# Eight weight operands of the second layer's MLP prepared one layer early and kept in DRAM

## The chip, the cores and the metric

The kernel runs on one core of one Trainium2 chip. Its time is the device time of one execution in microseconds (us). The comparison is between the medians of several executions; a profiled execution is a separate one.

## The reference

A trunk of two layers works on 1024 tokens of width 1024. Layer 0 mixes tokens by latent attention, layer 1 by a chunkwise mLSTM; each mixer is followed by a gated MLP. What the change touches is that MLP's first product, `h @ w_up`:

```
h = rms_norm(x) * (1 + sc_f) + sh_f
a, g = split(h @ w_up, 2)                 # w_up: 1024 x 5632, a and g 2816 wide
a = causal_depthwise_conv3(a) + conv_b
x = x + g_f * ((gelu(a) * g) @ w_down)
```

Everything is float32.

## The kernel before

**Three matmuls for one product.** A float32 operand is split in two: `hi`, its rounding to the fp32r format, made by ScalarE (ACT, line 1019), and `lo`, the rest, made by VectorE (DVE, line 1020). `mm3` (lines 178 to 180) adds up hi by hi, hi by lo and lo by hi on TensorE (PE).

**Seven products for eight.** An up pass (`mlp`, called once for each layer) works on 22 groups `m`. A group has 128 columns of `a` and 128 of `g`; the tokens come in two halves and the inner dimension in two halves, so a plain scheme has eight block products. The kernel uses seven, in a form with sums and differences of blocks. They are numbered 1 to 7: `p1` to `p7` run them, `w_a`, `w_s1`, `w_s3`, `w_s4` and small lambdas (together `weights_of`) make their weight operands. Operand 1 and 2 are the two halves of the `a` weights (`ra`) as they are; 5 is the sum of the halves of the `g` weights (`rg`, line 1033); 3, 6 and 7 derive from sums and differences (lines 1039, 1040, 1044); 4 is a half of `rg`. One product is 12 matmuls of 128x128 by 128x512. The seven activation operands are called B11, B21 (these come straight from `h`), T1, B22, T2, T3 and T4; the last five come from `operands_second`, whose DVE work is on lines 937, 969, 977, 981, 987 and 944.

**Order.** `sequence` lists the products as items. The first eight items of a pass are the operands 1 and 2 of groups 0 to 3 (`AHEAD = 4`), since their activations are ready first; then come 5, 5, 3, 3, 6, 6, 7, 7 of groups 0 and 1, then 5, 5, 4, 4 and so on. A loop at the end of `mlp` makes operands ahead of the product that runs: up to `LOOK` = 7 items ahead for the first eight and 5 after that. Since groups 0 to 3 come back later for operands that need `ra`, they load it again (`again`). The order of instructions on each engine is laid down at compile time by a planner with its own costs: it goes by the order of the program and fills an engine's gap with later work that it takes to be ready. At run time each engine keeps that order.

**Buffers.** Operands live in pairs in tiles `w0` and `w1` (hi and lo); there are four such tiles (`wbufs`), so eight operands. A tile comes free when both of its products have run. Raw weights have five tiles `raw`, the sums two tiles `wsum`.

**Stores for later.** In layer 0's up pass, between its products, 28 items make the weight operands of layer 1's output projection (four groups of seven) and write hi and lo to DRAM (`spill_units`, `wo_d`, by SyncE's (SP) queue); `SPILL = (47, 21)` puts them in four lots of seven, the first at item 47, with 21 products between two lots. Their raw weights and sums live in four rooms of one tile `sp`. Also from item 28 on, at every fourth item, `extra` does one of 24 dot products of the modulation (line 216).

**Where layer 1's up pass begins.** `OutProj` reads its stored operands back by GpSimd's queue (POOL, line 1373), two lots of products ahead, into the same `w0`/`w1` tiles. After its last products (`oa`) come layer 1's up products at once (`pa`, `pb`, `pd`). A few matmuls into them PE forms the sum of squares of the second half of the tokens (`st`, line 268), DVE and POOL make the reciprocal root of it (`rstd`, line 273), PE spreads it over the partitions (`rb`, line 280), and then `operands_second` can begin.

Of the kernel before, what the change touches and what calls it, by code (L numbers as in the profile page):

```python
# [11 lines left out]
F32 = mybir.dt.float32  # L12
F32R = mybir.dt.float32r
# [5 lines left out]
P = 128  # L19
# [4 lines left out]
HS = 512  # L24
# [63 lines left out]
U_MV0 = (U_MV, U_MV + 1, U_MG)  # L88
# [12 lines left out]
def trunk_kernel(ctx: ExitStack, tc: tile.TileContext, xT, pos, c_d, cols_d, mod_w, win, winT, w0, w1, wf, wd, out):  # L101
# [4 lines left out]
    def nm(s):  # L106
        n_names[0] += 1
        return f"{s}_{n_names[0]}"
# [23 lines left out]
    def block(i, shape, dt, name):  # L132
        return blk.tile(shape, dt, tag=f"b{i}", name=nm(name))
# [758 lines left out]
    def store_x(l, hf, m, x):  # L892
        nc.sync.dma_start(x_d[l][hf][m], x[:, m, :])
# [99 lines left out]
    def home(px, i, dt, name):  # L993
        return (px if i > 5 else blk).tile([P, KT, HS], dt, tag=f"b{i}", name=nm(name))

    def mlp(px, psC, T, l, u_d, pd, done, cols, extra=None, scaled=None, store=None, more=None, spill=None, homes=(6, 0)):

# [23 lines left out]
        def weights_of(raw, room_for=None):  # L1023

            def w_a(g):
                g["ra"] = raw(g["m"], 0)
                return wop(g["ra"][:, 0:HS], dve)

            def w_s1(g):
                g["rg"] = raw(g["m"], 1)  # L1030
                t = room_for() if room_for else wp.tile([P, 1024], F32, tag="wraw", bufs=wraws, name=nm("wsum"))
                g["s"], g["t"] = t[:, 0:HS], t[:, HS:]
                dve.tensor_tensor(g["s"], g["rg"][:, 0:HS], g["rg"][:, HS:], ALU.add)
                return wop(g["s"], dve)

            def w_s4(g):
                if g["again"]:
                    g["ra"] = raw(g["m"], 0)
                dve.tensor_tensor(g["s"], g["s"], g["ra"][:, 0:HS], ALU.subtract)
                dve.tensor_tensor(g["t"], g["ra"][:, HS:], g["s"], ALU.subtract)  # L1040
                return wop(g["t"], dve)

            def w_s3(g):
                dve.tensor_tensor(g["t"], g["ra"][:, 0:HS], g["rg"][:, 0:HS], ALU.subtract)
                return wop(g["t"], dve)

            return {1: w_a, 2: lambda g: wop(g["ra"][:, HS:], dve), 3: w_s4, 4: lambda g: wop(g["rg"][:, HS:], dve),
                    5: w_s1, 6: lambda g: wop(g["s"], dve), 7: w_s3}

        def prod(ps, w, t, first, T=T):  # L1050
# [69 lines left out]
        def sequence(groups, made, run):  # L1120
# [5 lines left out]
            for n in range(AHEAD, len(groups)):  # L1126
# [5 lines left out]

        seq = sequence([{"m": m, "again": m < AHEAD} for m in range(FT)], weights_of(raw),
                       {1: p1, 2: p2, 3: p3, 4: p4, 5: p5, 6: p6, 7: p7})
        if spill is not None:
            rooms = []

            def room_for():
                if not rooms:
                    t = block(2, [P, 4, 1024], F32, "sp")  # L1140
                    rooms.extend([t[:, i, :] for i in range(4)])
                rooms.append(rooms.pop(0))
                return rooms[-1]

            made = weights_of(lambda m, i: spill[0](room_for(), m, i), room_for)
            for n, g in enumerate({"m": m, "again": False} for m in range(4)):
                at = SPILL[0] + n * (SPILL[1] + 7)
                seq[at:at] = [(lambda k=k, g=g: made[k](g), lambda w, k=k, g=g: spill[1](k, g["m"], w))
                              for k in (1, 2, 5, 3, 6, 7, 4)]
        ends = {k: len(seq) - 1 - i for i, k in enumerate((4, 7, 6, 3, 0, 2, 0, 1, 5))}  # L1150
        hooks = {}

# [181 lines left out]

    REST = (7, 8, 10)
    DOTS = 28
    SPILL = (47, 21)
    pF = []
    ORD = (("B11", "B21", "T1", "B22", "T2", "T3", "T4"),) * 2 + (("B11", "T1", "T2", "B22", "T3", "B21", "T4"),)

# [147 lines left out]
    def mixer_products(weights_of, prod, bank, sequence, hook):  # L1488

        def unit_raw(m, i):  # L1490
            t = px.tile([P, 1024], F32, tag="raw", bufs=RAWS, name=nm("raw"))
            nc.sync.dma_start(t, w1[PAIRS[m][i]])
            return t

        def held(tag, shape, bufs):
            return pD[0].tile(shape, F32, tag=tag, bufs=bufs, name=nm("c"))[:, 0:HS]

        def scale_of(g):
            return KSCALE if g["m"] < MH else 1.0

        def result(g, row, hf, t):
            u = PAIRS[g["m"]][row]
            if u >= U_MO:
                og_form(t)
                nc.sync.dma_start(og_d[u - U_MO][hf], t)
            else:
                nc.sync.dma_start(qk_d[g["m"]][row][hf], t)

        def p1(g, w):
            g["A"] = mm_tile("ma")  # L1510
            prod(g["A"], w, "B11", True, hT)
            g["a1"] = held("raw1", [P, 1024], 4)
            with tc.high_priority():
                act.activation(g["a1"], g["A"], AF.Copy)

        def p2(g, w):
            b = bank("mb")
            prod(b, w, "B21", True, hT)
            with tc.high_priority():
                dve.tensor_tensor(g["a1"], g["a1"], b, ALU.add)  # L1520
            result(g, 0, 0, g.pop("a1"))

        def p5(g, w):
            g["D"] = bank("md")
            prod(g["D"], w, "T1", True, hT)
            g["g2"] = held("g2", [P, HS], 2)
            with tc.high_priority():
                act.activation(g["g2"], g["D"], AF.Copy, scale=scale_of(g))

        def p3(g, w):  # L1530
            prod(g["D"], w, "B22", False, hT)
            g["a2"] = held("raw1", [P, 1024], 4)
            with tc.high_priority():
                act.activation(g["a2"], g["D"], AF.Copy)

        def p6(g, w):
            prod(g["A"], w, "T2", False, hT)
            with tc.high_priority():
                dve.tensor_tensor(g["a2"], g["a2"], g["A"], ALU.add)
            result(g, 0, 1, g.pop("a2"))  # L1540

        def p7(g, w):
            prod(g["A"], w, "T3", False, hT)
            with tc.high_priority():
                dve.scalar_tensor_tensor(g["g2"], g["A"], scale_of(g), g["g2"], ALU.mult, ALU.add)
            result(g, 1, 1, g.pop("g2"))

        def p4(g, w):
            prod(g["A"], w, "T4", False, hT)
            t = held("raw1", [P, 1024], 4)  # L1550
            with tc.high_priority():
                act.activation(t, g["A"], AF.Copy, scale=scale_of(g))
            result(g, 1, 0, t)

        def b12():
            t = block(1, [P, KT, HS], F32R, "B12")
            hT["B12"] = t[:, 0:4], t[:, 4:8]
            for k in (0, 2):
                r = px.tile([P, 1024], F32, tag="raw", bufs=RAWS, name=nm("raw")).rearrange("p (k t) -> p k t", k=2)
                for i in range(2):  # L1560
                    nc.sync.dma_start(r[:, i, :], b12_d[k + i])
                split_two(hT["B12"], k, r)

        vps = []

        def v_first(j, w):
            if j == 0:
                need(hT["B11"])
                vps.extend(mm_tile("vf") for _ in range(4))
            for k in range(3 * j, min(3 * j + 3, KT)):  # L1570
                for t in range(4):
                    mm3(vps[t][:, 0:264], [x[:, k, t * P:(t + 1) * P] for x in hT["h"]], wk(w, k % 3, 264),
                        k == 0, k == KT - 1)
            if j == 2:
                v = pD[0].tile([P, 1024], F32, tag="raw1", bufs=4, name=nm("v"))
                with tc.high_priority():
                    for t in range(4):
                        act.activation(v[:, t * 256:(t + 1) * 256], vps[t][:, 0:256], AF.Copy)
                        dve.tensor_copy(gtok[:, :, t], vps[t][:, 256:264])
                nc.sync.dma_start(va_d, v)  # L1580

        n = len(PAIRS)
        for i in REST:
            hook(i + 3, lambda: (need(hT["T1"]), piece(hT["rest"])))
        hook(n * 7 - 2, b12)
        return [(lambda j=j: unit(w1[U_MV0[j]]), lambda w, j=j: v_first(j, w)) for j in range(3)] + sequence([{"m": m, "again": m < AHEAD} for m in range(n)], weights_of(unit_raw),
                        {1: p1, 2: p2, 3: p3, 4: p4, 5: p5, 6: p6, 7: p7})

    pD = []
    mlp(px, psC, T, 0, u_d[0], pD, done, ((0, HS),), lambda i: piece(mods, i >= DOTS and i % 4 == 0),  # L1590
        store=lambda hf, m, x: store_x(1, hf, m, x), more=mixer_products, spill=spill_units(1, w1, U_OUT1))
    for _ in mods:
        pass

# [366 lines left out]
    def done(hf, t0, w, x, ssq):  # L1961
# [2 lines left out]

    pD = []
    mlp(px, psC, T, 1, u_d[1], pD, done, ((0, 256), (256, 256)), lambda i: piece(mods, i >= 60 and i % 6 == 0), gain,
        homes=(0, 6))
    need(xs)
    stP.close()
    pD[1].close()  # L1970
# [98 lines left out]
```

## Time and profile before

| | |
|---|---|
| median of three executions | 2167.46 us (2167.31 to 2170.86) |
| the profiled execution's own time | 2169.14 us |
| its span, first to last instruction | 2167.4 us |
| PE busy | 2134.8 us, 98% of the span |
| DVE busy | 1770.3 us, 82% |
| ACT busy | 1078.4 us, 50% |
| POOL busy | 71.2 us, 3% |

The profile gives for each engine the time in which it had an instruction in work. PE's matmuls overlap, so a busy PE can still run below its pace; the number of matmuls in a stretch tells that. In a row of the view of the instructions in order of time there stand the start, the duration, the engine, the line, the operation, the tiles written and read, the shapes, the count, and in brackets how long the engine had been idle and what ended that. In the view by windows a row has the stretch and its length, then for each engine the busy time and the number of instructions, then the granted share of TensorE's clock, the busy share of the DMA engines and the GB/s that they moved.

### The profile page before, as it was taken

How to read it: one execution, taken by the hardware profiler on the slowest of the kernel's cores; microseconds unless marked ns; L12 is line 12 of the kernel's file. 1: busy time of each engine (PE TensorE's matmuls, PEld its weight loads, DVE VectorE, ACT ScalarE, POOL GpSimd, SP SyncE). 2: the span in 40 equal slices, each digit the busy share in tenths (PEclk: the TensorE clock that was granted, in tenths of full speed). 3: DMA queues.
4: the chain of work that ended last, by engine and by line, in shares of the span. 5: the costliest groups of instructions: out<-in, count | busy, mean ns of one | idle time of the engine just before them, and what ended most of it. 6: DMA issues, size and time to landing. Idle time of an engine off the chain costs nothing.

```text
span 2167.4 us, 28571 instructions
## 1 busy us (share of the span) xinstructions
PE 2134.8 (98%) x10401; PEld 1792.1 (83%) x10401; DVE 1770.3 (82%) x2837; ACT 1078.4 (50%) x1797; POOL 71.2 (3%) x164
## 2 busy tenths in 40 slices
PE   9999999999999999999999999999999999999998
PEld 7878888787888888878888889988788888887887
DVE  8877778669899987899988477787986777779988
ACT  5465566446555554433365464445644444453335
POOL 0000000000000000000000011021000000000000
PEclk9999999999999999999999999999999999999999
DMA  8512334842466652552144444486233332246212
GB/s 321 165 45 58 98 101 151 271 142 90 141 225 228 228 204 88 187 179 81 59 165 149 157 151 151 144 291 224 77 133 97 112 125 90 77 156 220 66 54 78
DMA packets 130700, 313.23 MB, mean 145 GB/s; under 512 B 14528, under 2 KB 22272, under 8 KB 130560
## 3 DMA queue, kind: packets, MB, share of 16 engines
q1 hardware_dynamic: 126128, 296.33, 41.3%
q0 software_dynamic: 4032, 14.68, 2.1%
q8 instruction: 82, 1.34, 0.3%
q14 instruction: 58, 0.48, 0.1%
q10 hardware_dynamic: 400, 0.39, 0.1%
HBM read 242.24 MB, written 65.96 MB: 142 GB/s over the span
## 4 chain that ended last, share of the span: by engine, by line
PE 84%; DVE 7%; DMA 4%; issue 2%; ACT 2%; SPq 1%; POOL 1%; POOLq 0%; DVEq 0%; ACTq 0%
PE pa L178 7%; PE pa L180 7%; PE pa L179 7%; PE pd L180 4%; PE pd L178 4%; PE pd L179 4%; PE sc L698 4%; PE da L178 3%; PE da L179 3%; PE da L180 3%; PE db L178 2%; PE db L180 2%; PE db L179 2%; PE pb L180 2%; PE pb L178 2%
## 5 line engine op out<-in xcount | busy, mean ns | idle before, releaser
L178 PE MATMUL pa<-T,whi 128*128 128x512 f32 x528 | 206.0, 390 | 0.0
L179 PE MATMUL pa<-T,whi 128*128 128x512 f32 x528 | 205.6, 389 | 0.0
L180 PE MATMUL pa<-T,wlo 128*128 128x512 f32 x528 | 205.2, 389 | 0.0
L1019 ACT ACTIVATE whi<-wsum 128x512 fp32r<-128x512 f32 x196 | 120.1, 626 | 137.6 <-PE pa L179 53.1
L1020 DVE TENSOR_TENSOR wlo<-wsum,whi 128x512 fp32r<-128x512 f32 x196 | 132.1, 686 | 29.8 <-ACT whi L1019 28.3
L179 PE MATMUL da<-U,whi 128*128 128x512 f32 (+1 forms) x364 | 139.1, 382 | 0.0
L178 PE MATMUL da<-U,whi 128*128 128x512 f32 (+1 forms) x364 | 139.1, 382 | 0.0
L1019 ACT ACTIVATE whi<-raw 128x512 fp32r<-128x512 f32 x147 | 88.7, 623 | 101.3 <-PE pb L179 49.4
L180 PE MATMUL da<-U,wlo 128*128 128x512 f32 (+1 forms) x364 | 138.7, 382 | 0.0
L1238 ACT ACTIVATE whi<-raw 128x1024 fp32r<-128x1024 f32 (+1 forms) x60 | 59.2, 987 | 133.5 <-PE da L179 56.8
L1020 DVE TENSOR_TENSOR wlo<-raw,whi 128x512 fp32r<-128x512 f32 x147 | 99.6, 686 | 23.8 <-ACT whi L1019 23.8
L178 PEld LDWEIGHTS pa<-T,whi 128*128 128x128 f32 x528 | 99.2, 188 | 21.8 <-DVE a L1105 0.7
L180 PEld LDWEIGHTS pa<-T,wlo 128*128 128x128 f32 x528 | 99.3, 188 | 20.7
L179 PEld LDWEIGHTS pa<-T,whi 128*128 128x128 f32 x528 | 99.2, 188 | 20.6
L1064 ACT ACTIVATE ct<-a,cols 128x512 f32<-128x512 f32 x88 | 70.9, 810 | 80.2 <-DVE a L1086 46.1
L180 PE MATMUL db<-U,wlo 128*128 128x512 f32 x264 | 102.7, 390 | 1.7 <-DVE wlo L1239 1.7
L178 PE MATMUL db<-U,whi 128*128 128x512 f32 x264 | 103.3, 391 | 0.8 <-ACT whi L1238 0.8
L179 PE MATMUL db<-U,whi 128*128 128x512 f32 x264 | 102.9, 390 | 0.0
L1189 ACT ACTIVATE U<-q 128x1024 fp32r<-128x1024 f32 x84 | 79.9, 979 | 45.4 <-DMA q<-ud 15.9
L1190 DVE TENSOR_TENSOR U<-q,U 128x1024 fp32r<-128x1024 f32 x84 | 94.2, 1130 | 5.3 <-ACT U L1189 5.3
L1065 DVE SCALAR_TENSOR_TENSOR ct<-a,cols,ct 128x512 f32<-128x512 f32 x88 | 65.6, 748 | 18.4 <-ACT ct L1064 18.4
L178 PEld LDWEIGHTS da<-U,whi 128*128 128x128 f32 x364 | 68.4, 188 | 13.9 <-ACT whi L1238 0.7
(486 smaller groups left out, 6231.1 us busy)
## 6 DMA issues: line engine op xcount, KB each, us to landing
raw<-in_wf SPq DMA_DIRECT2D x96, 512.0 KB, 4.2
mraw<-in_mod_w SPq DMA_DIRECT2D x56, 512.0 KB, 4.1
wraw<-in_w SPq DMA_DIRECT2D x44, 512.0 KB, 3.5
ud<-ct SPq DMA_DIRECT2D x88, 256.0 KB, 2.1
q<-ud SPq DMA_DIRECT2D x88, 256.0 KB, 4.7
raw<-in_wd SPq DMA_DIRECT2D x32, 512.0 KB, 4.2
pa<-in_mod_w SPq DMA_DIRECT2D x24, 512.0 KB, 3.6
x<-xd SPq DMA_DIRECT2D x48, 256.0 KB, 4.6
```

The lines of the kernel that those rows point to most:

```text
L178: pe.matmul(ps, lh, rh, start=first, stop=False, skip_group_check=more)
L179: pe.matmul(ps[:, 0:rl.shape[-1]], lh, rl, start=False, stop=False, skip_group_check=more)
L180: pe.matmul(ps, ll, rh, start=False, stop=last, skip_group_check=more)
L698: pe.matmul(ps[:, cs], a[:, qs if n < 3 else qrs_], b[:, cs], start=n == 0, stop=n == 4)
L1019: act.activation(hi, src, AF.Copy)
L1020: eng.tensor_tensor(lo, src, hi.bitcast(F32), ALU.subtract)
L1064: act.activation(t, a[:, 2:], AF.Identity, bias=col(f"cb{l}", m), scale=cw(m, 2))
L1065: dve.scalar_tensor_tensor(t, a[:, 1:HS + 1], cw(m, 1), t, ALU.mult, ALU.add)
L1189: act.activation(hi, w, AF.Copy)
L1190: dve.tensor_tensor(lo, w, hi.bitcast(F32), ALU.subtract)
L1238: act.activation(hi, src, AF.Copy)
```

## The change

Operands 1 and 2 of groups 0 to 3 of layer 1's up pass, its first eight items, are no longer made there. They are made in layer 0's up pass as eight more items (36 in all) and stored in DRAM (`ff_d`, by `ff_store`); layer 1 reads them back by POOL's queue (`ff_first`), two operands at a time into one pair of tiles. The 36 items come in six lots of six, the first at item 42, with 14 products between two lots; the four groups of seven are now cut across the lots, and the eight new items come last. The raw weights of the new items come into the same four rooms of `sp`. `w_g2` loads `rg` where a group has not loaded it; here every group that uses operand 4 has. What stands as `seq = ...; return seq` in `mixer_products` is only written differently.

```diff
+        if first is not None:
+            seq[:len(FIRST)] = [(lambda i=i: first(i), seq[i][1]) for i in range(len(FIRST))]
         if spill is not None:
-            rooms = []
...
-            made = weights_of(lambda m, i: spill[0](room_for(), m, i), room_for)
-            for n, g in enumerate({"m": m, "again": False} for m in range(4)):
-                at = SPILL[0] + n * (SPILL[1] + 7)
-                seq[at:at] = [(lambda k=k, g=g: made[k](g), lambda w, k=k, g=g: spill[1](k, g["m"], w))
-                              for k in (1, 2, 5, 3, 6, 7, 4)]
+            items = list(spilled(weights_of, spill[:2], 2, spill[2]))
+            for n in range(SPILL[2]):
+                m = len(items) // SPILL[2]
+                at = SPILL[0] + n * (SPILL[1] + m)
+                seq[at:at] = items[n * m:n * m + m]
...
-    SPILL = (47, 21)
+    SPILL = (42, 14, 6)
+    FIRST = [(k, m) for m in range(4) for k in (1, 2)]
...
+    def ff_load(t, m, i):
+        nc.sync.dma_start(t, wf[1, m, i])
+        return t
+
+    def ff_store(k, m, hl):
+        i = FIRST.index((k, m))
+        for d, v in zip(ff_d[i // 2], hl):
+            nc.sync.dma_start(d[:, i % 2 * HS:(i % 2 + 1) * HS], v.bitcast(F32))
+
+    def up_spill():
+        load, store = spill_units(1, w1, U_OUT1)
+        ff = sorted(FIRST, key=lambda x: (x[1], (1, 2, 5, 3, 6, 7).index(x[0])))
+        items = [(k, m) for m in range(4) for k in (1, 2, 5, 3, 6, 7, 4)] + [(k, m + 4) for k, m in ff]
+        return (lambda t, m, i: load(t, m, i) if m < 4 else ff_load(t, m - 4, i),
+                lambda k, m, w: store(k, m, w) if m < 4 else ff_store(k, m - 4, w), items)
+
+    def ff_first(i):
+        if i % 2 == 0:
+            w = [wp.tile([P, 1024], F32R, tag=f"w{j}", bufs=wbufs, name=nm(f"w{j}")) for j in ("hi", "lo")]
+            for v, d in zip(w, ff_d[i // 2]):
+                nc.gpsimd.dma_start(v, d.bitcast(F32R))
+            for j in range(2):
+                ff_w[i + j] = [v[:, j * HS:(j + 1) * HS] for v in w]
+        return ff_w[i]
...
-        store=lambda hf, m, x: store_x(1, hf, m, x), more=mixer_products, spill=spill_units(1, w1, U_OUT1))
+        store=lambda hf, m, x: store_x(1, hf, m, x), more=mixer_products, spill=up_spill())
...
-        homes=(0, 6))
+        homes=(0, 6), first=ff_first)
```

`spilled` holds the old code of the rooms, for a list of items that may cut groups.

More of the change, by code (lines that the diff above doesn't have):

```diff
@@ L994, in home, with mlp @@
         return (px if i > 5 else blk).tile([P, KT, HS], dt, tag=f"b{i}", name=nm(name))
-    def mlp(px, psC, T, l, u_d, pd, done, cols, extra=None, scaled=None, store=None, more=None, spill=None, homes=(6, 0)):
+    def mlp(px, psC, T, l, u_d, pd, done, cols, extra=None, scaled=None, store=None, more=None, spill=None, homes=(6, 0), first=None):
         cw = lambda m, j: col(f"cw{l}", m * 3 + j)
@@ L1045, in w_s3, with w_g2 @@
                 return wop(g["t"], dve)
-            return {1: w_a, 2: lambda g: wop(g["ra"][:, HS:], dve), 3: w_s4, 4: lambda g: wop(g["rg"][:, HS:], dve),
+            def w_g2(g):
+                if "rg" not in g:
+                    g["rg"] = raw(g["m"], 1)
+                return wop(g["rg"][:, HS:], dve)
+            return {1: w_a, 2: lambda g: wop(g["ra"][:, HS:], dve), 3: w_s4, 4: w_g2,
                     5: w_s1, 6: lambda g: wop(g["s"], dve), 7: w_s3}
@@ L1134, in mlp @@
                        {1: p1, 2: p2, 3: p3, 4: p4, 5: p5, 6: p6, 7: p7})
+        if first is not None:
+            seq[:len(FIRST)] = [(lambda i=i: first(i), seq[i][1]) for i in range(len(FIRST))]
         if spill is not None:
-            rooms = []
[L1138 to L1143, printed above, removed]
-            made = weights_of(lambda m, i: spill[0](room_for(), m, i), room_for)
-            for n, g in enumerate({"m": m, "again": False} for m in range(4)):
-                at = SPILL[0] + n * (SPILL[1] + 7)
-                seq[at:at] = [(lambda k=k, g=g: made[k](g), lambda w, k=k, g=g: spill[1](k, g["m"], w))
-                              for k in (1, 2, 5, 3, 6, 7, 4)]
+            items = list(spilled(weights_of, spill[:2], 2, spill[2]))
[3 more added lines that the diff above has]
+                seq[at:at] = items[n * m:n * m + m]
         ends = {k: len(seq) - 1 - i for i, k in enumerate((4, 7, 6, 3, 0, 2, 0, 1, 5))}
@@ L1336, in trunk_kernel, with spilled, room_for @@
     DOTS = 28
-    SPILL = (47, 21)
+    SPILL = (42, 14, 6)
+    FIRST = [(k, m) for m in range(4) for k in (1, 2)]
+    def spilled(weights_of, spill, home, items):
+        rooms, groups = [], {}
+        def room_for():
+            if not rooms:
+                t = block(home, [P, 4, 1024], F32, "sp")
+                rooms.extend([t[:, i, :] for i in range(4)])
+            rooms.append(rooms.pop(0))
+            return rooms[-1]
+        made = weights_of(lambda m, i: spill[0](room_for(), m, i), room_for)
+        for k, m in items:
+            g = groups.setdefault(m, {"m": m, "again": False})
+            yield (lambda k=k, g=g: made[k](g)), (lambda w, k=k, m=m: spill[1](k, m, w))
+    ff_d = [[dram.tile([P, 1024], F32, name=f"ff{i}{j}") for j in "hl"] for i in range(len(FIRST) // 2)]
+    ff_w = {}
+    def ff_load(t, m, i):
[19 more added lines that the diff above has]
+        return ff_w[i]
     pF = []
@@ L1585, in mixer_products @@
         hook(n * 7 - 2, b12)
-        return [(lambda j=j: unit(w1[U_MV0[j]]), lambda w, j=j: v_first(j, w)) for j in range(3)] + sequence([{"m": m, "again": m < AHEAD} for m in range(n)], weights_of(unit_raw),
+        seq = [(lambda j=j: unit(w1[U_MV0[j]]), lambda w, j=j: v_first(j, w)) for j in range(3)]
+        seq += sequence([{"m": m, "again": m < AHEAD} for m in range(n)], weights_of(unit_raw),
                         {1: p1, 2: p2, 3: p3, 4: p4, 5: p5, 6: p6, 7: p7})
+        return seq
     pD = []
     mlp(px, psC, T, 0, u_d[0], pD, done, ((0, HS),), lambda i: piece(mods, i >= DOTS and i % 4 == 0),
-        store=lambda hf, m, x: store_x(1, hf, m, x), more=mixer_products, spill=spill_units(1, w1, U_OUT1))
+        store=lambda hf, m, x: store_x(1, hf, m, x), more=mixer_products, spill=up_spill())
     for _ in mods:
```

## Prediction

> **What bounds the kernel now.** I read the page's busy times first, then windows of 100 us, then PE's waits, then the instructions in order of time where PE waits.
>
> ```profile
> PE 2134.8 (98%) x10401; PEld 1792.1 (83%) x10401; DVE 1770.3 (82%) x2837; ACT 1078.4 (50%) x1797; POOL 71.2 (3%) x164
> ```
> ```profile
> 600.00:700.00 100.00, 100.00 (x443) 82.80 (x442) 93.99 (x158) 52.12 (x88) 0.50 (x5) 1.00 0.69 232
> ...
> 1500.00:1600.00 100.00, 95.46 (x419) 78.07 (x418) 95.73 (x134) 65.12 (x98) 1.69 (x4) 0.97 0.32 109
> ```
> ```profile
> PE pd L178 <- ACT whi L1019: 4.3, 1, 4.3
> PE rb L280 <- POOL rstd L273: 0.2, 1, 0.2
> ```
>
> PE bounds nearly everywhere: 443 matmuls in 100 us is one each 0.226 us, so 2.71 us for a product of 12. Layer 0's up pass keeps that pace between 600 and 700 although DVE is 94% busy there. Layer 1's up pass starts badly (419 matmuls between 1500 and 1600). The last two rows are all of PE's waits from 1490 to 1960 us. Here is that place, PE first, then DVE:
>
> ```profile
> 1513.48 0.39 PE L178 MATMUL pa<-h,whi 128*128 128x512 f32 x1
> ...
> 1516.89 0.28 PE L268 MATMUL st<-ones,ssq 128*128 128x1 f32 x2
> ...
> 1561.50 0.79 PE L178 MATMUL pd<-T,whi 128*128 128x512 f32 x1 [4.31 <-ACT whi L1019]
> ...
> 1566.69 0.39 PE L180 MATMUL pa<-T,wlo 128*128 128x512 f32 x1
> ```
> ```profile
> 1518.77 0.16 DVE L272 TENSOR_SCALAR var<-st 128x4 f32<-128x4 f32 x1 [1.65 <-PE st L268]
> 1518.85 2.48 DVE L1020 TENSOR_TENSOR wlo<-raw,whi 128x512 fp32r<-128x512 f32 x4
> 1521.25 1.21 DVE L937 TENSOR_TENSOR x<-x,rb 128x1024 f32<-128x1024 f32 x1
> ...
> 1530.25 0.68 DVE L1033 TENSOR_TENSOR wsum<-raw 128x512 f32<-128x512 f32 x1
> ...
> 1557.23 0.69 DVE L1112 TENSOR_TENSOR g<-g,pa 128x512 f32<-128x512 f32 x1
> 1557.83 2.35 DVE L944 TENSOR_TENSOR T<-x,T 128x1024 fp32r<-128x1024 f32 x2
> 1560.10 1.29 DVE L1033 TENSOR_TENSOR wsum<-raw 128x512 f32<-128x512 f32 x2
> ```
> ```profile
> 1521.00:1557.00 36.00, 36.00 (x160) 29.61 (x159) 35.39 (x42) 24.97 (x34) 0.00 (x0) 1.00 0.22 82
> ```
> ```profile
> 1559.83:1566.63 6.80, 5.13 (x11) 3.64 (x12) 6.79 (x13) 4.76 (x8) 0.00 (x0) 0.50 0.00 0
> ```
>
> PE waits for item 16 (operand 5 of group 2), whose sum is the L1033 at 1560.10. DVE made it so late because it worked without a break from 1521.25 on (35.39 of 36 us): when `rb` is there, `operands_second` and the operands of items 8 to 15 come in one heap. After the wait PE runs at half clock (0.50): from 1561.50 to the twelfth start at 1566.69, eleven steps, it takes 5.19 us instead of 11 x 0.226 = 2.49. So this place costs 0.23 + 4.31 + 2.70 = 7.24 us. That is all there is to win, 0.33% of the time.
>
> **The change part by part.**
>
> *Removed in layer 1: eight hi (ACT), eight lo (DVE), four loads of raw weights (SP).* A lo costs DVE 0.60 us (the four at 1518.85 in 2.48, overlapping), so 4.8 us go. But where? They lie before 1521.25, and the heap behind begins with L937, which needs `rb`:
>
> ```profile
> 1514.72 1.14 ACT L1019 ACTIVATE whi<-raw 128x512 fp32r<-128x512 f32 x2
> 1515.77 0.62 ACT L247 ACTIVATE sq<-x 128x512 f32<-128x512 f32 x1
> ```
> ```profile
> 1522.30 0.63 ACT L1019 ACTIVATE whi<-wsum 128x512 fp32r<-128x512 f32 x1 [5.30 <-PE pb L179]
> ```
> ```profile
> 1490.63 0.53 POOL L1373 DMA_DIRECT2D whi<-wo1T42h  x1 [4.33 <-PE oa L180]
> ```
> ```profile
> 1519.01 1.39 POOL L273 TENSOR_TENSOR rstd<-var,nhalf 128x4 f32<-128x4 f32 x1 [22.22 <-DVE var L272]
> ```
>
> `rb` waits for POOL's `rstd` (until 1520.40), that for `st`, and `st` stands in PE's order. So 4.8 us of DVE leave a stretch in which DVE then only waits longer. What does get out of the heap: (a) one L1033. At 1530.25 stands the sum of group 1; its raw weights needed a `raw` tile that the first operands held, and DVE's free time went to their lo. Now five `raw` tiles are free for rg0, rg1, ra0, ra1, rg2, and the sum can be made before `rb`: 0.60 us. The other operands of the heap can't move up: item 8's hi waits for a tile `w0` until the second product is done (the 5.30 at 1522.30), and so do all after it, before and after the change. (b) `st`. The program asks for it four steps of `mm3`, 12 matmuls, after 1513.48, that is at 1516.20; it stands at 1516.89, one step later, as the last square (L247) came late behind four hi on ACT. Without these I take it one step earlier, 0.68 us (bounds 0 and 0.68). Together the heap moves by 1.28 us and the wait of 4.31 becomes 3.03.
>
> The half clock: PE then restarts at 1560.22. A much shorter gap was also followed by such a stretch:
>
> ```profile
> 1366.39 0.38 PE L178 MATMUL po<-va,pT 128*128 128x258 f32 x1 [1.32 <-DVE C L1737]
> ```
> ```profile
> 1368.68:1372.08 3.40, 3.40 (x13) 2.91 (x12) 3.40 (x8) 1.17 (x4) 0.00 (x0) 0.50 0.53 148
> ```
>
> A gap of 1.32 us gave 3.40 us at half clock, that of 4.31 gave 6.80. For 3.03 I take one such stretch, 1559.83 to 1563.23; PE works in 3.0 us of it and loses half, 1.5 (bounds 0 and 2.70). New cost 0.23 + 3.03 + 1.5 = 4.76; gain 7.24 - 4.76 = 2.48 us.
>
> [...]
>
> *Added in layer 1: eight loads by POOL of 512 KB.* An issue takes 0.53 us (row 1490.63), eight 4.3. A pair waits for its `w0` tile, as `oa`'s did (4.33 idle). The last pair's tile comes free with the last `oa` product at 1513.48, so its issues end by 1514.6; queued behind them is `rstd` at 1519.01, 4.4 us later. Landing:
>
> ```profile
> DMA to landing us min/median/max: 3.6/6.6/11.2
> ```
>
> Even 11.2 us brings the last pair at 1525.8, and its products, the seventh and eighth, run from about 1532. Cost 0; cover gone only if a landing takes over 17 us. Four loads fewer on SP help nobody who is late.
>
> *Added in layer 0: eight hi, eight lo, four loads of `ra`, 16 stores on SP.* ACT 8 x 0.57 = 4.6 us (two in 1.14, row 1514.72), DVE 4.8 us, on engines beside PE. 70 products lie between the six lots, 190 us, and DVE at 94% has room for 11 us there. SP issues 20 more DMAs. Behind SP's waiting stores stand raw loads for later products, and behind a late operand PE. The lot itself is the tight place; the first of the old lots, ACT, DVE, PE:
>
> ```profile
> 594.83 0.63 ACT L1019 ACTIVATE whi<-wsum 128x512 fp32r<-128x512 f32 x1 [1.89 <-PE pa L179]
> ```
> ```profile
> 612.21 0.69 DVE L1020 TENSOR_TENSOR wlo<-wsum,whi 128x512 fp32r<-128x512 f32 x1
> ```
> ```profile
> 613.84 0.39 PE L178 MATMUL pd<-T,whi 128*128 128x512 f32 x1
> ```
> ```profile
> 638.12 0.69 DVE L1020 TENSOR_TENSOR wlo<-wsum,whi 128x512 fp32r<-128x512 f32 x1
> ```
>
> From 594.83, when a tile came free, to 612.90, when the first operand behind the lot was ready, nine operands were made (the one before the lot, seven, the one behind): 2.0 us each, bounded by tiles coming free. PE wanted it at 613.84: 0.94 us to spare, and no wait. A lot of six that starts at an even item has three full pairs: seven operands from its first free tile, 14.1 us at that rate, and PE has six products, 16.3 us. So 2.2 us to spare, more than now. Behind a lot the margin came back: fourteen products on, at 613.84 + 14 x 2.71 = 651.8, PE used the operand that was ready at 638.8 (row 638.12, the fourteenth lo behind that at 612.21, those of the next lot left out), 13 us ahead. 14 products between lots are thus just enough. Cost 0; bounds 0 and, if two lots miss, 9 us (below).
>
> *The sum:* 2167.4 - 2.48 = 2164.9 us of span. The profiled execution took 2169.14, 1.7 us more than its span and than the median of 2167.46; taken from the median, 2165.0 us. A difference under 0.2%, 4.3 us, can't be told from none here.
>
> **The rivals.**
>
> *The heap is reordered (faster).* In layer 0 the same heap cost PE less, since DVE's order had the two L1033 ahead of the last L944 of T4:
>
> ```profile
> 488.24 2.35 DVE L937 TENSOR_TENSOR x<-x,rb 128x1024 f32<-128x1024 f32 x2 [2.46 <-PE rb L280]
> ```
> ```profile
> 524.16 1.29 DVE L1033 TENSOR_TENSOR wsum<-raw 128x512 f32<-128x512 f32 x2
> ```
>
> From L937 to the end of the sums were 37.2 us there, 40.1 in layer 1. If the planner, whose gaps move, puts one L944 (1.14 us) and L1112 (0.60) behind the sums, the wait falls from 3.03 to 1.3 and the half clock to 0.5 or so: 7.24 - 0.23 - 1.8 = 5.2 us, 2162.3. For it: layer 0. Against: the operands ahead of the sums have the earlier place in the program. Chance 0.32.
>
> [...]
>
> *The lots break (slower).* In the third and fourth lot the groups are cut so that `rg` needs a room that comes free in the same lot. Its load is then inside the lot; loads into `sp` landed after:
>
> ```profile
> DMA to landing us min/median/max: 3.7/5.9/7.1
> ```
>
> The lot's third pair starts about 5 us after the first, so the sum waits 1 to 2 us, of the 2.2 to spare. If SP holds the load behind a store for 3 us more, two lots miss by 3 us each, and each miss over about 1.3 us brings 1.5 us of half clock: 9 us, less 2.5: 2174. It decides from about 2 us of delay on. For it: DVE at 94% and the margin of 0.94. Against: smaller lots. Chance 0.15.
>
> *Nothing moves in layer 1*, since DVE's order and `st` stay: 2167.4; 0.13.
>
> **How the numbers follow.** My forecast has 0.35, and the rivals 0.32, 0.05, 0.15 and 0.13. Faster by over 0.2% is the reordered heap but for its weaker half, and a little of the forecast: 0.28. Slower is the lots: 0.14. The rest, 0.58, is within 0.2%. The range runs from 2161 (reordered, with no more than 0.9 of the 7.24 left) to 2172 (one lot misses, 3 + 1.5 us, and nothing is won); the forecast's own range is 2163.5 (no clock lost) to 2166.9 (no step of `st`, and the clock's 2.70 stays).
>
> **What would show it.** Right: PE's wait for ACT's hi of line 1019 at the start of layer 1's up pass shrinks to about 3 us; no lo from raw stands between `var` and the first L937; the L1033 of group 1 lies before `rb`; `st` is 12 matmuls behind the first `pa`; PE keeps 443 matmuls in 100 us from 600 to 800 with no new wait. Wrong: L1033 of group 2 stands ahead of T4's L944 and the wait is near 1 us; or PE waits behind a lot; or POOL's loads land after PE wants them.

## The result and the profile after

The changed kernel took 2163.85 us (median of 12 runs, 2160.20 to 2166.48), the kernel before 2168.59 us beside it (12 runs, 2166.06 to 2172.38). The ratio is 0.9977, 95% interval 0.9969 to 0.9985: faster by 0.23%, 4.74 us between the medians. That is inside the range of the prediction, and about twice its gain of 2.48 us. The profiled spans are 2161.5 us after and 2167.4 us before, 5.9 us apart.

The lines after answer to those of before in the prediction. In the changed file the lines that the prediction calls 1065, 1098 and 1112 are 1070, 1103 and 1117; 937, 944, 1019, 1020 and 1033 kept their numbers. First the busy times of the page, then windows of 100 us (length, then busy time of PE, PEld, DVE, ACT and POOL with instructions, granted clock, DMA share, GB/s):

```profile
PE 2130.5 (99%) x10401; PEld 1787.5 (83%) x10401; DVE 1770.3 (82%) x2837; ACT 1077.6 (50%) x1797; POOL 75.1 (3%) x172
```
```profile
600.00:700.00 100.00, 99.31 (x439) 81.92 (x438) 97.30 (x166) 51.32 (x87) 0.50 (x5) 1.00 0.73 250
700.00:800.00 100.00, 99.59 (x440) 82.15 (x439) 89.71 (x151) 53.16 (x90) 0.50 (x5) 1.00 0.73 254
...
1500.00:1600.00 100.00, 98.92 (x443) 80.60 (x443) 94.19 (x131) 63.94 (x96) 4.67 (x14) 1.00 0.42 140
```

DVE does as much as before, 1770.3 us, and POOL has eight instructions more. The stretch from 1500 to 1600 has 443 matmuls where it had 419, at a clock of 1.00 instead of 0.97. Between 600 and 800 us, where the kernel before had no wait, 439 and 440 stand for 443. PE's waits in layer 0's up pass (530 to 900 us), then at layer 1's (1490 to 1960 us):

```profile
PE pa L178 <- ACT whi L1019: 0.7, 1, 0.7
PE pa L178 <- DVE g L1117: 0.4, 1, 0.4
```
```profile
PE pd L178 <- ACT whi L1019: 0.9, 1, 0.9
PE db L180 <- DVE wlo L1237: 0.6, 1, 0.6
```

So 4.31 us at item 16 became 0.94, and two waits behind lots are new. The wait at `db` is not: before, it was 0.86 us at 1965.78, just outside the stretch of that view. The place in order of time, PE and then DVE, and what PE did in the 6.80 us after its wait:

```profile
1513.22 0.39 PE L178 MATMUL pa<-h,whi 128*128 128x512 f32 x1
...
1515.62 0.38 PE L268 MATMUL st<-ones,ssq 128*128 128x1 f32 x2
...
1557.64 0.50 PE L178 MATMUL pd<-T,whi 128*128 128x512 f32 x1 [0.94 <-ACT whi L1019]
...
1560.83 0.39 PE L179 MATMUL pd<-T,whi 128*128 128x512 f32 x1
```
```profile
1517.61 0.16 DVE L272 TENSOR_SCALAR var<-st 128x4 f32<-128x4 f32 x1 [2.04 <-PE st L268]
1519.97 2.35 DVE L937 TENSOR_TENSOR x<-x,rb 128x1024 f32<-128x1024 f32 x2 [2.20 <-PE rb L280]
...
1554.75 1.22 DVE L987 TENSOR_TENSOR x<-x 128x1024 f32<-128x1024 f32 x1
1555.89 1.29 DVE L1033 TENSOR_TENSOR wsum<-raw 128x512 f32<-128x512 f32 x2
1557.09 0.68 DVE L1117 TENSOR_TENSOR g<-g,pa 128x512 f32<-128x512 f32 x1
1557.69 1.22 DVE L944 TENSOR_TENSOR T<-x,T 128x1024 fp32r<-128x1024 f32 x1
```
```profile
1557.64:1564.44 6.80, 6.65 (x27) 4.94 (x28) 6.79 (x12) 3.71 (x6) 0.00 (x0) 1.00 0.00 0
```

The reader is to see three things. Between `var` and L937 DVE now waits, where it made four lo. Behind the two L1033 of item 16's group stand one L944 and the addition to `g` that stood ahead of them before. And no half clock follows: 27 matmuls in 6.80 us at a clock of 1.00, where there were 11 (at full pace there would be 30). From 1557.64 to the twelfth start at 1560.83, eleven steps, PE takes 3.19 us, 0.70 more than at full pace.

Counted from the first `pa`, the first of these L1033 starts at 1555.89 - 1513.22 = 42.67 us; before at 1560.10 - 1513.48 = 46.62. Of these 3.95 us, 1.02 are an earlier L937 (6.75 against 7.77 us behind the first `pa`); 2.93 are a shorter run from L937 on. That run has 41 instructions instead of 44: without the L1033 of group 1 (0.60), one L944 (1.14) and the addition to `g` (0.60), 2.34 us together; of the other 0.6 us, 0.4 are shorter gaps (DVE worked 38.19 of 38.85 us before and 35.63 of 35.92 after) and 0.2 slightly shorter steps.

### The profile page after: what moved, and what is told of

Read it like the earlier page. It is cut to its first block, busy times and chain, and to the rows that moved or that the text cites. A ratio compares the mean times of both kernels' runs of the same rounds, so it can differ in the third digit from the quotient of the medians.

```text
span 2161.5 us, 28617 instructions
## 1 busy us (share of the span) xinstructions
PE 2130.5 (99%) x10401; PEld 1787.5 (83%) x10401; DVE 1770.3 (82%) x2837; ACT 1077.6 (50%) x1797; POOL 75.1 (3%) x172
## 4 chain that ended last, share of the span: by engine, by line
PE 82%; DVE 8%; DMA 5%; issue 2%; ACT 2%; SPq 1%; POOL 1%; DVEq 0%; POOLq 0%; ACTq 0%
PE pa L178 6%; PE pa L180 6%; PE pa L179 6%; PE sc L698 4%; PE da L178 3%; PE da L180 3%; PE da L179 3%; PE pd L180 3%; PE pd L178 3%; PE pd L179 3%; PE db L180 2%; PE db L178 2%; PE db L179 2%; PE pb L180 2%; PE pb L178 2%
## 5 line engine op out<-in xcount | busy, mean ns | idle before, releaser
L1019 ACT ACTIVATE whi<-raw 128x512 fp32r<-128x512 f32 x139 | 84.2, 623 | 92.5 <-PE pb L179 45.1
L1020 DVE TENSOR_TENSOR wlo<-raw,whi 128x512 fp32r<-128x512 f32 x139 | 94.3, 686 | 22.3 <-ACT whi L1019 21.8
L1072 ACT ACTIVATE ct<-ct 128x512 f32<-128x512 f32 x88 | 55.0, 627 | 50.5 <-DVE ct L1071 50.2
```

Of the source, the lines that this page charges most:

```text
L1019: act.activation(hi, src, AF.Copy)
L1020: eng.tensor_tensor(lo, src, hi.bitcast(F32), ALU.subtract)
L1072: act.activation(t, t, AF.Gelu)
```

## The experiments

The theory after the result was that VectorE's backlog from the first L937 to the sums of item 16 sets the wait, by its start and by its order. The rival was that the wait shrinks by the amount of work taken away, wherever it is taken. Every ratio is to the kernel before, run on the same chip.

**1. Layer 0's part alone.** Lots of 36 operands, but layer 1 makes its eight operands as before.

```diff
-        homes=(0, 6), first=ff_first)
+        homes=(0, 6))
```

> Layer 0 makes and stores all 36 items in six lots as in the changed kernel; layer 1 makes its first eight operands itself, as in the kernel before (the stored eight are not read). Theory H (the gain is all at the start of layer 1's up pass; the new lots cost a little): 1 to 2 us slower than the kernel before, with PE waits of 0.4 to 0.7 us behind lots between 630 and 770 us, and at the start of layer 1's up pass the old wait of 4.3 us with half clock behind it. Rival L (the new lots are what helps, or are free): same as before or faster, no PE wait behind a lot.

Measured: 1.0006 [0.9997, 1.0014], 2170.57 us. Layer 1's start is that of before:

```profile
PE pd L178 <- ACT whi L1019: 4.3, 1, 4.3
PE pd L180 <- DVE wlo L1020: 0.5, 1, 0.5
PE rb L280 <- POOL rstd L273: 0.2, 1, 0.2
```

A wait of 0.4 us and one of 0.2 us in layer 0 are new. A price of 1.3 us for the lots is the best guess of this run, and no price lies within its interval too.

**2. Layer 1's part alone.** The old four lots of seven; the tensors in DRAM are filled by copies of raw weights, so the split of those eight operands is left out.

```diff
-    SPILL = (42, 14, 6)
+    SPILL = (47, 21, 4)
...
+    def ff_copy(i):
+        if 0 <= i < len(FIRST):
+            nc.sync.dma_start(ff_d[i // 2][i % 2], wf[1, i // 2, 0])
...
```

> Layer 0 makes 28 items in four lots of seven as before; the DRAM copies that layer 1 reads are filled by plain DRAM to DRAM copies of the raw weights in layer 0's up pass, so hi and lo of these eight operands are not split (this part of the computation is left out). Theory H: 5 to 7 us faster than the kernel before, 1 to 2 us faster than the changed kernel; PE's wait at the start of layer 1's up pass is 0.9 us and no stretch at half clock follows. Rival L: less than 3 us faster than before.

Measured: 0.9974 [0.9963, 0.9985], 2163.41 us, with the same wait of 0.94 us at item 16. So the gain is layer 1's, and the 5.6 us of this ratio lie in the range that the theory gave. That this run should be 1 to 2 us below the changed kernel can't be seen.

**3. The order alone.** In the kernel before, T4 of layer 1 is made at item 11 instead of 10, so that more of its L944 fall behind the sums.

```diff
-        for i in REST:
+        for i in REST if l == 0 else (7, 8, 11):
```

> The kernel before, with nothing moved between the layers; only in layer 1 the operand T4 is asked for at item 11 instead of 10, so that in DVE's order the sum of group 2 (L1033) stands ahead of T4's four instructions. Theory H, of which DVE's order is a part: the wait of 4.3 us falls to 2 us or less, half clock mostly gone, 3 to 6 us faster than the kernel before. Rival W (it is the amount of work taken off layer 1 that counts, not the order): same as before, within 1 us.

Measured: 0.9993 [0.9983, 1.0003], 2166.93 us: the expected 3 to 6 us did not come. VectorE's rows show why; the first `pa` was at 1516.19:

```profile
1556.95 0.69 DVE L1033 TENSOR_TENSOR wsum<-raw 128x512 f32<-128x512 f32 x1
...
1562.83 0.69 DVE L1033 TENSOR_TENSOR wsum<-raw 128x512 f32<-128x512 f32 x1
```
```profile
1564.58 0.50 PE L178 MATMUL pd<-T,whi 128*128 128x512 f32 x1 [1.43 <-ACT whi L1019]
1565.97 0.50 PE L180 MATMUL pd<-T,wlo 128*128 128x512 f32 x1 [0.66 <-DVE wlo L1020]
1579.28 0.50 PE L178 MATMUL pd<-B,whi 128*128 128x512 f32 x1 [1.43 <-ACT whi L1019]
```

Item 16's sum came 40.76 us behind the first `pa`, but item 17's at 46.64, where both stood before. PE no longer waited at item 16 and reached item 17 earlier, to wait there 1.43 and 0.66 us, and half clock followed. A later T4 shifts the stall by one item.

**4. The order undone.** The changed kernel with T4 of layer 1 one item earlier.

```diff
-        for i in REST:
+        for i in REST if l == 0 else (7, 8, 9):
```

> The changed kernel, only in layer 1 T4 is asked for at item 9 instead of 10, so that both L944 of T4 and the gate's addition stand ahead of the two L1033 in DVE's order, as in the kernel before. Theory H: PE's wait at item 16 grows from 0.94 to about 2.7 us and a stretch at half clock follows, so 2.5 to 4.5 us slower than the changed kernel. Rival W: as fast as the changed kernel, within 1 us.

Measured: 0.9984 [0.9975, 0.9994], 2165.53 us. Both sums stand 44.43 us behind the first `pa` (1557.11 - 1512.68), 1.76 later than in the changed kernel: the L944 and the addition are back ahead of them. The wait, and the windows row behind it:

```profile
1558.51 0.50 PE L178 MATMUL pd<-T,whi 128*128 128x512 f32 x1 [2.35 <-ACT whi L1019]
```
```profile
1559.65:1563.06 3.41, 3.41 (x9) 2.69 (x9) 3.41 (x8) 2.36 (x4) 0.00 (x0) 0.50 0.00 0
```

The wait grew by 1.41 us and a stretch at half clock came back, nine matmuls for fifteen. In time that is 1.5 us (0.9984 against 0.9977), less than the 2.5 to 4.5 expected, and the intervals overlap; in the trace it is plain.

**5 and 6. Half of the operands.** As the second run (the old four lots, copies of raw weights), with four operands from DRAM: the last four, or the first four. Only the line that differs is shown.

```diff
-            seq[:len(FIRST)] = [(lambda i=i: first(i), seq[i][1]) for i in range(len(FIRST))]
+            seq[4:8] = [(lambda i=i: first(i), seq[i][1]) for i in range(4, 8)]
```
```diff
+            seq[:4] = [(lambda i=i: first(i), seq[i][1]) for i in range(4)]
```

> Layer 1's part alone, as in the second experiment, but with only the fifth to the eighth of the eight operands read from DRAM; the first four are made at their places. As there, the operands in DRAM are copies of raw weights, so the split of them is left out. Theory H (what counts is when VectorE's backlog from the first L937 to the two L1033 of item 16's group ends, that is its start and the order in it): the four `lo` that VectorE still makes all lie ahead of `var` in the program's order, the backlog keeps the order of the changed kernel, and TensorE's wait at item 16 is 0.9 to 1.6 us with no half clock behind it: 0.9970 to 0.9982 of before. Rival W (only the amount of work taken from VectorE and ScalarE counts): half the operands bring half the gain, a wait near 2.6 us, 0.9985 to 0.9990. Rival P (nothing of the eight counts, the gain of the second experiment came from the lots that are left out): 0.9970 to 0.9978 with the wait at any size.

> The counterpart: only the first four operands are read from DRAM (copies of raw weights again), the fifth to the eighth are made at their places. Two `lo` stand between `var` and the first L937 in the program's order, and ahead of L1033 of item 16's group one L944 less is let past than in the kernel before. Theory H: the backlog starts 0.6 to 1.2 us later than in the changed kernel, the wait at item 16 is 2.0 to 3.5 us and one half-clock stretch of about 1.7 us follows: 0.9985 to 0.9998 of before. Rival W: as the last four, 0.9985 to 0.9990 with a wait near 2.6 us; so it is the difference between this run and the last four (H 1.5 to 5 us, W none) that tells the two apart.

Measured: last four 0.9984 [0.9975, 0.9993], 2165.45 us; first four 0.9975 [0.9967, 0.9984], 2162.93 us. PE's waits there, last four and then first four:

```profile
PE pd L180 <- DVE wlo L1020: 0.9, 1, 0.9
PE pd L178 <- ACT whi L1019: 0.9, 1, 0.9
```
```profile
PE pd L178 <- ACT whi L1019: 0.7, 1, 0.7
PE pa L178 <- DVE g L1117: 0.4, 1, 0.4
PE rb L280 <- POOL rstd L273: 0.3, 1, 0.3
```

Neither has half clock there (from 1500 to 1600 us the clock is 1.00 in both). The theory had the first four worse, by a later start of the backlog; their waits were the shorter ones, so it fell on this point; the time of the last four, too, lies just above the theory's 0.9970 to 0.9982. The intervals of the two runs overlap. The rival's waits of 2.6 us fell as well: four operands take nearly all of the stall, whichever four. The first L1033 of the sums stands 42.38 and 43.03 us behind the first `pa` (1556.28 - 1513.90; 1557.20 - 1514.17).

**7. The start of the backlog put back.** The changed kernel with the sums `st` two steps later.

```diff
-    O_WAIT, O_RSTD = (6, 3), (4, 3)
+    O_WAIT, O_RSTD = (6, 5), (4, 3)
```

> The changed kernel with the sums `st` of layer 1's norm two steps of TensorE's order later (O_WAIT from (6, 3) to (6, 5)), which puts them about where they stood in the kernel before; DRAM operands and lots unchanged. Theory H: the backlog starts some 0.7 to 1.2 us later, its length and the order of its end stay, the wait at item 16 grows from 0.94 to 1.6 to 2.2 us and one half-clock stretch (1.7 us) comes back: 1 to 3 us above the changed kernel, 0.9982 to 0.9991 of before. Rival (the place of the sums is hidden, the gain is the order's alone): wait 0.9 to 1.1 us and the changed kernel's time, 0.9972 to 0.9982.

Measured: 0.9984 [0.9975, 0.9993], 2165.14 us: by the ratios 1.5 us above the changed kernel, with overlapping intervals. The first `pa`, the start of the backlog, its sums, and PE's two waits with the windows row that begins at the first:

```profile
1514.96 0.39 PE L178 MATMUL pa<-h,whi 128*128 128x512 f32 x1
```
```profile
1523.71 4.60 DVE L937 TENSOR_TENSOR x<-x,rb 128x1024 f32<-128x1024 f32 x4
...
1557.10 0.68 DVE L1033 TENSOR_TENSOR wsum<-raw 128x512 f32<-128x512 f32 x1
1561.18 0.68 DVE L1033 TENSOR_TENSOR wsum<-raw 128x512 f32<-128x512 f32 x1
```
```profile
1558.85 0.50 PE L178 MATMUL pd<-T,whi 128*128 128x512 f32 x1 [0.61 <-ACT whi L1019]
1561.31 0.50 PE L180 MATMUL pd<-T,wlo 128*128 128x512 f32 x1 [0.94 <-DVE wlo L1020]
```
```profile
1558.85:1565.68 6.83, 5.80 (x23) 4.23 (x24) 6.82 (x12) 2.72 (x5) 0.00 (x0) 1.00 0.00 0
```

The backlog starts 8.75 us behind the first `pa`, even later than in the kernel before (7.77), and yet the first sum stands at 42.14. Up to it are only 38 instructions for 44: the L1033 of group 1 and the addition to `g` are out of it as in the changed kernel, two L944 instead of one have gone behind the sum, and one other addition and one lo ahead of L937. So the start of the backlog does not set the wait by itself; with a later start the program's order put more work behind the first sum. The half clock that the theory expected did not come: the time lies in its range, the mechanism that it gave is not in the trace.

**8. Lots 16 apart, and T4 later.** The changed kernel with both edits: a try at a better one. SPILL holds the item before which the first lot stands, the items between two lots and the number of lots.

```diff
-        for i in REST:
+        for i in REST if l == 0 else (7, 8, 11):
-    SPILL = (42, 14, 6)
+    SPILL = (42, 16, 6)
```

> The changed kernel with the lots 16 items apart instead of 14 (second and third number of SPILL (42, 16, 6)) and, in layer 1, T4 drained one item later, at item 11 (its L944 behind item 16's additions). Theory H: the wait of 0.94 us at item 16 goes, up to 0.9 us of it comes back at items 17 to 20, and the lots meet other evictions: their waits of 0.69 and 0.41 us go or move; 0 to 2 us below the changed kernel, 0.9968 to 0.9978 of before. Rival (as with T4 later in the kernel before, the wait only moves to items 17 and 20 and half clock follows it): 0.9978 to 0.9990.

Measured: 0.9983 [0.9975, 0.9992], 2164.81 us; not better. Layer 1 behaved (its largest wait 0.9 us, the clock 1.00 from 1500 to 1600 us), but PE's waits in layer 0 grew:

```profile
PE pa L178 <- DVE g L1117: 3.3, 4, 1.2
```

**9. Nine lots of four.** Layer 1 untouched.

```diff
-    SPILL = (42, 14, 6)
+    SPILL = (42, 8, 9)
```

> The changed kernel with its 36 operands made in nine lots of four, 8 items apart, in place of six lots of six, 14 apart (SPILL (42, 8, 9)); layer 1 is untouched. What is disputed is the price of the lots in layer 0. Theory L (a lot of more operands than there are tile pairs makes the operand behind it wait for a store): the waits of 0.69 and 0.41 us of the changed kernel go and no new one above 0.3 us comes, the excess of its two places (1.6 us) goes with them: 0.9967 to 0.9977 of before, 0 to 2 us below the changed kernel. Rival M (a lot costs by where it meets layer 0's evictions, as the lots 16 apart did): 1 to 4 waits of 0.3 to 1.2 us at `pa <- g`, 0 to 3 us above the changed kernel: 0.9978 to 0.9992. Layer 1's wait at item 16 stays at 0.94 us in both.

Measured: 1.0007 [0.9998, 1.0016], 2170.93 us: the rival won, and by more than it said. Layer 1 keeps its 0.9 us, but layer 0's up pass has six waits of 6.9 us together, in an execution that took 3.6 us more than the median. The waits, then one of them, and the windows row of the half clock behind it:

```profile
PE pa L178 <- DVE g L1117: 4.1, 4, 2.2
PE pa L178 <- ACT whi L1019: 2.8, 2, 1.4
```
```profile
766.21 0.47 PE L178 MATMUL pa<-T,whi 128*128 128x512 f32 x1 [2.18 <-DVE g L1117]
```
```profile
767.69:771.10 3.41, 3.41 (x10) 2.67 (x9) 3.38 (x7) 1.29 (x2) 0.00 (x0) 0.50 0.89 331
```

Against the 1.1 us of waits in the changed kernel that is 5.8 us more, and half of 3.41 for the clock: 7.5 us; the ratios are 6.5 us apart (0.0030 of 2168.6). The place of the lots in layer 0 can thus undo the whole gain.

**10. The change with four operands.** The first four, split in layer 0 and read back, nothing left out; 32 operands in eight lots of four.

```diff
-    SPILL = (42, 14, 6)
-    FIRST = [(k, m) for m in range(4) for k in (1, 2)]
+    SPILL = (42, 10, 8)
+    FIRST = [(k, m) for m in range(2) for k in (1, 2)]
```

> The change with four operands instead of eight (the first four, split in layer 0 and read back, nothing left out), 32 operands in eight lots of four, 10 items apart. After the experiments before it the theory reads: what counts in layer 1 is how long after the first `pa` the first L1033 of item 16's group stands (46.6 us before, 44.4 with T4 one item earlier, 42.1 to 43.0 in the runs without a half-clock stretch), and four operands move it as far as eight. Expected: first L1033 at 42 to 43.5 us, waits of 0.4 to 0.9 us at items 16 and 17, no half clock there, 0.9968 to 0.9982 of before. Rival (the eight are needed, the half copies' run was helped by the missing lots): a wait over 2 us with half clock, 0.9985 to 0.9998.

Measured: 0.9978 [0.9969, 0.9987], 2164.95 us. The first L1033 at 1556.53 - 1513.50 = 43.03 us, PE's waits there and in layer 0:

```profile
PE pd L178 <- ACT whi L1019: 0.7, 1, 0.7
PE pa L178 <- DVE g L1117: 0.4, 1, 0.4
PE rb L280 <- POOL rstd L273: 0.3, 1, 0.3
```
```profile
PE pa L178 <- DVE g L1117: 0.8, 2, 0.5
```

As expected on every point, and without half clock there (1.00 from 1500 to 1600 us). Half of the change brings what the whole brings, as far as this measurement tells them apart. None of these ten kernels beats the changed one by more than its interval.

What the runs say together, in us behind the first `pa`:

| run | first, second L1033 | waits of PE there | half clock behind |
|---|---|---|---|
| before; 1 | 46.6, 47.2 | 4.31 (run 1: and 0.47) | 6.8; run 1: 3.4 |
| 3 | 40.8, 46.6 | 1.43 + 0.66, later 1.43 | 3.4 |
| 4 | 44.4, 45.0 | 2.35 | 3.4 |
| after; 2; 9 | 42.7, 43.3 | 0.94 (run 9: and 0.15) | after and 9: none |
| 5 | 42.4, 46.5 | 0.86 + 0.94 | none |
| 6; 10 | 43.0, 46.0 | 0.7 + 0.4 | none |
| 7 | 42.1, 46.2 | 0.61 + 0.94 | none |
| 8 | 38.0, 42.7 | 0.86 and 0.16, at later items | none |

With both sums together, each us that the first stands later adds 0.8 to 0.9 us of wait (0.94 at 42.7, 2.35 at 44.4, 4.31 at 46.6), and half clock followed at 2.35 us and not at 0.94. With the sums apart, as in 5, 6, 7 and 10, the stall splits in two short waits and costs no clock; in run 3, with waits of 2.09 us together against run 5's 1.80, it did, though its second sum stands only 0.2 us later than run 5's; no run shows what sets these two apart. Why the wait at 1579.28 arose there is open.

## Why the prediction was right in the number and wrong in the way

The time came as forecast, in the range and near the 2165.0 us; the way was the rival called "the heap is reordered", which had 0.32 and 2162.3 us, against 0.35 for the forecast. That the time is so near is in part luck: the kernel before took 2168.59 us beside it and not the 2167.46 that the forecast counts from. The gain, 4.74 us, is nearer to the rival's 5.2 than to the forecast's 2.48. A gain over 0.2% had been given only 0.28; and a difference under 0.2% was called too small to tell, while this interval reaches only 0.08% to either side.

*What bounds the kernel* was right: the place cost 7.24 us, and what the change won came from there. Measured in the same way, it costs 1.64 after: 0.94 of wait and 0.70 in the eleven steps behind it.

*(a) One L1033 leaves the backlog, 0.60.* Right: none of group 1 stands in it any more, and no lo from raw lies between `var` and L937.

*(b) `st` one step earlier, 0.68.* Mis-sized. I read the program as asking for four steps; (6, 3) asks for three. `st` stands 2.40 us behind the first `pa` instead of 3.41, and L937 moved by 1.02. And it was not needed: in run 7 the start was later than before and the stall was gone all the same.

*The order stays.* This is the step that failed. One L944 and the addition to `g`, 1.14 + 0.60 = 1.74 us, went behind the sums, and with that the prediction's own sign of being wrong came: the sums ahead of T4's last L944 and a wait near 1 us. With the 0.34 that (b) was short, this is 2.08 us, and the forecast wait (3.03) and the measured one (0.94) are 2.09 apart. The two agree so well because what is left nearly cancels: the 0.6 us of gaps and shorter steps make the sums earlier still, while PE came 0.23 us earlier to its wait (before, it had waited for `rb`) and needed 1.75 instead of 1.40 us from the start of the sums to item 16's first matmul. Run 4, where the two are back ahead of the sums, has 2.35 us and half clock: near the forecast's own picture. I had weighed this rival by the place of the instructions in the program; the row of layer 0 (37.2 us from L937 to the end of the sums) was the better guide. After, it is 1519.97 to 1557.18 = 37.21 us in layer 1.

*Half clock 1.5 us.* None came behind 0.94 us. Run 4, with a wait of 2.35 us, had such a stretch, nine matmuls for fifteen; so for a wait of 3.03 the term was a fair estimate. The 2163.5 us in the forecast's own range counts no clock lost behind that wait. No run shows this: none had a wait of that length in layer 1's up pass, and half clock came behind the longer 4.31 us (the kernel before) as behind the shorter 2.35 us (run 4).

*The sum.* 7.24 - 1.64 = 5.60 us won in layer 1. The profiled spans agree: from the first `pa` to the end are 653.9 us before and 648.3 after, 5.6 apart. Up to the first `pa` the changed kernel is only 0.26 us ahead, and in that stand, among smaller differences, two opposite things: in layer 0's up pass it fell back by 1.7 us (counted in PE's order, its matmul at 635.5 came 1.00 us earlier than in the kernel before, that at 773.2 came 0.67 later), and the kernel before alone had the stretch at half clock at 1368.68, which no run ties to the change. Without that stretch, 5.60 us won and 1.7 lost make 3.9 us, within the interval of the ratio (3.3 to 6.7 us).

*POOL's eight loads cost nothing.* Right, with the tile's release as the prediction had it:

```profile
1513.56 0.53 POOL L1377 DMA_DIRECT2D whi<-ff3h  x1 [4.33 <-PE oa L180]
1514.14 0.54 POOL L1377 DMA_DIRECT2D wlo<-ff3l  x1
1517.85 1.03 POOL L273 TENSOR_TENSOR rstd<-var,nhalf 128x4 f32<-128x4 f32 x1 [3.17 <-DVE var L272]
```

The last issue ends at 1514.68, and `rstd` waits for `var`, not for POOL. The eight loads landed 4.2 to 5.8 us after their issue.

*The lots cost nothing.* Wrong in the trace: 0.69 us at 643.61 and 0.41 us at 758.55, and 1.7 us of PE's time with the slower steps around them. The first of them comes from the second lot, where ACT's hi for the next product waits for a store to land:

```profile
639.18 0.63 ACT L1019 ACTIVATE whi<-wsum 128x512 fp32r<-128x512 f32 x1 [1.52 <-DMA wo1T20h<-whi]
```
```profile
643.61 0.47 PE L178 MATMUL pa<-T,whi 128*128 128x512 f32 x1 [0.69 <-ACT whi L1019]
```

I had counted seven operands at 2.0 us each and a spare of 2.2 us; the wait for the stores was not in it. In time run 1 can't tell it from nothing. But runs 8 and 9 show that the rival "the lots break" needed only another spacing; run 9 took 2170.93 us, with the gain in layer 1 kept, so an end near its 2174 us was possible.

## What to carry to other kernels

Where an engine works off a backlog and another waits for one item of it, ask first what stands ahead of that item and whether the planner will keep it so: here the order of two instructions moved the wait by 1.4 us and brought back half clock, while half of the operands removed did as much as all. If another layer of the same kernel has the same backlog with another order, take it as the likely outcome and not as a curiosity. Work that is made ahead in a full stage has its price in the spacing: the same operands cost nothing measurable in six lots of six and 6.5 us more in nine lots of four.

## What the runs showed of the hardware

In the places told of here the half clock came in stretches of 3.40 us (1368.68 in the kernel before) and 3.41 us (runs 3, 4 and 9), or of twice that (6.80 us at 1559.83 in the kernel before). Within one, PE's matmuls of 128x512 started 0.43 us apart instead of 0.23 (run 9: 768.07, 768.49, 768.92), and nine or ten stood in 3.41 us for fifteen. The distance from the first matmul behind the wait to the start of the stretch varied: in the kernel before it began 1.67 us ahead of it (1559.83 against 1561.50), in run 4 1.14 us behind it (1559.65 against 1558.51), in run 9 1.48 us behind it (767.69 against 766.21), and at 1368.68 in the kernel before 2.29 us behind it (1366.39).

In the up passes PE had been busy for 0.77 (before), 1.14 (run 4), 1.45 (run 3) and 1.48 us (run 9) in the 3.41 us ahead of the stretch; both waits of run 3, 1.43 and 0.66 us, end in those 3.41 us. In run 7 waits of 0.61 and 0.94 us, with PE busy for 1.86 us in the 3.41 up to the end of the second (1561.31), had none behind them: the clock stayed at 1.00. The rows of the kernel before, run 3 and run 9:

```profile
1556.42:1559.83 3.41, 0.77 (x4) 0.31 (x2) 3.36 (x4) 1.23 (x2) 0.00 (x0) 1.00 0.18 72
```
```profile
1563.28:1566.69 3.41, 1.45 (x5) 0.93 (x6) 3.41 (x6) 1.25 (x2) 0.00 (x0) 1.00 0.00 0
```
```profile
764.28:767.69 3.41, 1.48 (x7) 1.25 (x8) 3.41 (x6) 0.76 (x2) 0.00 (x0) 1.00 0.38 141
```

The length of a wait alone does not tell here whether half clock follows. At 1368.68 in the kernel before it followed a wait of 1.32 us, with PE busy for 2.13 us in the 3.41 ahead of it; at the same matmul the changed kernel waited 1.18 us and the 6.82 us behind it had a clock of 1.00. In run 9 a wait of 1.45 us had none behind it, and in run 3 after that of 1.43 us at 1579.28 the matmuls went on at full pace, 0.23 us apart. The kernel before, the changed one, and run 9 with its windows row:

```profile
1365.27:1368.68 3.41, 2.13 (x11) 1.56 (x12) 3.41 (x7) 1.63 (x6) 0.00 (x0) 1.00 0.50 169
```
```profile
1366.81 0.39 PE L178 MATMUL po<-va,pT 128*128 128x258 f32 x1 [1.18 <-DVE C L1782]
```
```profile
1366.81:1373.63 6.82, 6.64 (x39) 5.62 (x40) 6.82 (x15) 3.64 (x13) 0.00 (x0) 1.00 0.59 208
```
```profile
705.01 0.47 PE L178 MATMUL pa<-T,whi 128*128 128x512 f32 x1 [1.45 <-ACT whi L1019]
```
```profile
705.01:708.42 3.41, 3.41 (x15) 2.82 (x16) 3.41 (x7) 1.50 (x3) 0.00 (x0) 1.00 0.91 300
```

So the prediction's reading, one stretch behind each miss of over about 1.3 us, did not hold in run 9. What decides it no run here shows.
